# Output projection of the last 1024 rows by seven products in place of eight, behind the last attention step

## The chip, the cores and the metric

The kernel runs on one core of a Trainium2 chip (trn2). The metric is the device time of one execution in microseconds. TensorE is called PE, its weight loads PEld, VectorE DVE, ScalarE ACT, GpSimd POOL and SyncE SP. SP issues nearly all the DMAs of this kernel.

## The reference

One layer of an encoder: a norm, one input projection to queries, keys, values and a gate, a neighbourhood attention over a grid of 32 rows of 64 tokens, an output projection with a residual, and a last norm. All is float32.

```python
def rmsnorm(x, g):
    xf = x.astype(jnp.float32)
    y = xf * lax.rsqrt(jnp.mean(xf * xf, axis=-1, keepdims=True) + RMS_EPS)
    return (y * g.astype(jnp.float32)).astype(x.dtype)

# S = 2048 tokens, D = 1024, 16 heads of 64
h = rmsnorm(x, norm_0)
q, k, v, gate = jnp.split(h @ w_in_0, 4, axis=-1)
o = neighbourhood_attention(q, k, v, rpb_0)     # 8 x 16 neighbours, a bias per head and offset
x = x + (o * jax.nn.silu(gate)) @ w_out_0       # 2048 x 1024 by 1024 x 1024
out = rmsnorm(x, norm_f)
```

## The kernel before

A float32 matrix product is done in three matmuls: each operand is split into a high half h, which is the value rounded to the matmul's format (ACT copies), and a low half l = t - h (DVE subtracts), and h*h, h*l and l*h are added up in a PSUM bank. `split_to` (L433 to L439) does this.

The kernel has three parts.

1. Two stages project the input. They already multiply by seven products in place of eight: an operand is cut into four quarters, sums and differences of quarters are formed, and each of the seven products has 4 x 3 = 12 matmuls with 512 columns (`seven_products`, matmuls on L353). Several products accumulate into one bank, and DVE or ACT reads the bank out between them. POOL multiplies some results by the norm (L373).
2. The attention runs in 32 steps over (row group T, pair of heads p), `order` being T first. T is one of four groups of 512 token rows. In each step PE computes scores (s, L947), DVE adds the bias and takes the minimum of the negated score (L956), ACT takes the exponential (L961), POOL normalises (L970), PE turns the result (ph, L987), DVE and ACT copy it out (L990), PE multiplies by the values (o, L1006), and DVE multiplies by the gate (og, L1010). og is stored to a DRAM tile `ogd` and read back later with heads as rows.
3. While this chain goes on, PE is fed with other matmuls, here called fillers: `fill` (values of the second half, L846, 192 matmuls) and then `outs`, the output projection (po, L1226 to L1230). `feed(n)` takes n fillers at a time; `amount` holds how many are due in each of the steps. In the first ten steps it is 16 (with a shift between the first two), in the last 24, and in the others what the sum leaves. `feed(..., 8)` may borrow up to 4 fillers from the next step where row work was just issued (`calm`). What is left after the last step is run in a loop behind it, called the tail here.

The output projection takes 128 rows at a time (16 row tiles n) in two halves of 512 columns j: 8 k-blocks x 3 matmuls each, 48 matmuls per row tile. Around it, `load_og` reads a row tile of og, `split_og` splits it, `add_rows` adds the residual (L1108, DVE) and squares (L1111, ACT), and `finish` takes the root (L1124 DVE, L1125 and L1126 ACT), scales by root and gain (L1134, DVE) and sends the rows. The last head pair of the first two tiles of each T is not read back but split straight from og (`direct`, L1020).

Order: the program's order is written out by the code itself. `due(n)` moves a clock by matmuls, and `store(key, lag, f)` hands in work that is recorded when the clock is there. Each engine then runs its instructions in the recorded order and waits for semaphores; a DMA waits in SP's queue in the same way.

Of the kernel before, what the change touches and what calls it, by code (L numbers as in the profile page):

```python
# [23 lines left out]
NP = H // 2  # L24
# [36 lines left out]
def build(ctx, tc, x, xr, xt, wg, tab, w_out, n0, nf, out):  # L61
# [931 lines left out]
    def values(m):  # L993
# [29 lines left out]
        if p == lastp[T]:  # L1023
            store(("last", T), 2, direct)
# [60 lines left out]
    def add_rows(n, j, ps):  # L1085
        xr = RES.pop((n, j))
        state["event"] = clock[0]
        if j == 0:
            Y[n] = [], tiny.tile([128, 8], F32, name="st3")
        y, st = (raw if j else ev)([128, 512], F32, "y"), Y[n][1]  # L1090
        Y[n][0].append(y)
        if n == tiles - 1:
            cut = [slice(0, 256), slice(256, 512)] if j else [slice(0, 512)]
            for s in cut:
                nc.vector.tensor_tensor(y[:, s], ps[:, s], xr[:, s], OP.add)
            for k, s in enumerate(cut):
                to = st[:, (j if k == 0 else 5):(j if k == 0 else 5) + 1]
                nc.scalar.activation(xr[:, s], y[:, s], AF.Square, scale=0.5 ** 0.5, accum_out=to)
            if j == 0:
                nc.vector.tensor_scalar(st[:, 6:7], st[:, 0:1], 0.5 * D * EPS, None, op0=OP.add)  # L1100
            else:
                nc.vector.tensor_scalar(st[:, 7:8], st[:, 1:2], st[:, 6:7], None, op0=OP.add)
            w = (raw if j else ev)([128, 512], F32, "yw")
            nc.vector.tensor_tensor(w, y, late["nf"][j], OP.mult)
            Y[n][0][j] = w
            squared[0] += 1
            return
        nc.vector.tensor_tensor(y, ps, xr, OP.add)  # L1108

        def square():  # L1110
            nc.scalar.activation(xr, y, AF.Square, scale=0.5 ** 0.5, accum_out=st[:, j:j + 1])  # L1111
            squared[0] += 1

        store(("y", n, j), 5, square)

    def finish(n):
# [3 lines left out]
        def root():  # L1120
            if n == tiles - 1:
                nc.scalar.activation(h, st[:, 5:6], AF.Ln, bias=st[:, 7:8], scale=1.0)
            else:
                nc.vector.tensor_scalar(a, st[:, 0:1], st[:, 1:2], 0.5 * D * EPS, op0=OP.add, op1=OP.add)  # L1124
                nc.scalar.activation(h, a, AF.Ln)  # L1125
            nc.scalar.activation(r, h, AF.Exp, scale=-0.5)  # L1126

        def scale():
            if n == tiles - 1:
                nc.scalar.activation(y[0], y[0], AF.Copy, scale=r)  # L1130
                nc.vector.tensor_scalar(y[1], y[1], r, None, op0=OP.mult)
            else:
                for j in range(2):
                    nc.vector.scalar_tensor_tensor(y[j], y[j], r, late["nf"][j], op0=OP.mult, op1=OP.mult)  # L1134

        def send():
            for j in range(2):
                (nc.scalar if n == tiles - 1 and j == 0 else nc.sync).dma_start(
                    out[n * 128:n * 128 + 128, 512 * j:512 * j + 512], y[j])
# [100 lines left out]

    cycles = len(order)
# [9 lines left out]
    credit = [0.0]  # L1251
    alive = [True]

    def feed(n, calm=0):
        credit[0] += n
        while credit[0] > 0 or credit[0] > -calm_debt and clock[0] - state["event"] < calm:
# [11 lines left out]
            credit[0] -= got  # L1268
            due(got)
# [28 lines left out]
    for m in range(cycles + 1):  # L1298
# [15 lines left out]
        if m:  # L1314
            turns(m - 1)
        if m == cycles:
            all_loads()
# [13 lines left out]
    while next(outs, 0) != 0:  # L1331
        due(1)
    due(1e9)
# [31 lines left out]
```

## Time and profile before

| what | value |
|---|---|
| median of 3 runs | 1023.53 us (1023.42 to 1024.62) |
| profiled execution, its own time | 1023.25 us |
| its span, first to last instruction | 1021.4 us |
| mean granted clock of PE | 0.998 |
| PE busy | 1013.2 us, 8176 matmuls |
| DVE, ACT, POOL busy | 664.8, 474.3, 201.0 us |
| last o matmul of the attention ends | 966.06 us |
| last matmul ends | 1015.26 us |

Times are microseconds from the start of the span unless marked ns. A row of a timeline gives start, duration, engine, line, operation, output and inputs, shape and count, and in brackets the idle time before it and what ended it. Several like instructions in a row are merged to one row. A row of a group gives the count, the busy time and the mean duration in ns. A row of a stretch gives its length and each engine's busy time.

### The profile page before, as it was taken

What the parts mean: (1) busy time and instruction counts of PE and PEld (TensorE: products, weight loads), DVE (VectorE), ACT (ScalarE), POOL (GpSimd) and SP (SyncE); (2) the same over time, 40 slices, a digit from 0 to 9 for tenths busy, and PEclk for the clock granted to TensorE, in tenths of its full rate; (3) what the DMA queues carried; (4) which work ended last, traced back from release to release, by engine and by line L of the source; (5) the groups of instructions that cost most, each with busy time, mean ns of one, the idle gap of its engine ahead of it and who ended that gap; (6) DMA issues with size and microseconds to landing.
All of it is one profiled execution on the core that took longest, in us unless ns stands there. A gap on an engine that the chain in (4) does not pass through costs nothing.

```text
span 1021.4 us, 21642 instructions
## 1 busy us (share of the span) xinstructions
PE 1013.2 (99%) x8176; PEld 820.2 (80%) x8176; DVE 664.8 (65%) x1492; ACT 474.3 (46%) x1208; POOL 201.0 (20%) x341
## 2 busy tenths in 40 slices
PE   9999999999999999999999999999999999999997
PEld 7888888888888888888888877777777777877886
DVE  5385667678898795656555656667667665766543
ACT  7555323333325362332322356676666655666421
POOL 0000132232132310000000013444333332323200
PEclk9999999999999999999999999999999999999999
DMA  9633434453627244332334689899878787988442
GB/s 318 239 103 103 138 132 144 120 154 119 175 93 227 73 116 130 95 124 94 114 103 137 176 249 294 299 330 321 270 239 278 255 257 267 302 285 289 143 149 82
DMA packets 113344, 192.46 MB, mean 188 GB/s; under 512 B 10008, under 2 KB 44184, under 8 KB 113240
## 3 DMA queue, kind: packets, MB, share of 16 engines
q1 hardware_dynamic: 112808, 190.68, 58.3%
q8 instruction: 64, 1.05, 0.4%
q10 hardware_dynamic: 432, 0.40, 0.1%
q14 instruction: 40, 0.33, 0.1%
HBM read 140.71 MB, written 50.33 MB: 187 GB/s over the span
## 4 chain that ended last, share of the span: by engine, by line
PE 92%; DVE 6%; ACT 1%; issue 1%; DMA 0%; DVEq 0%; ACTq 0%
PE pp L353 42%; PE pv L477 9%; PE o L1006 8%; PE s L947 6%; PE po L1226 6%; PE po L1230 6%; PE po L1228 6%; PE ph L987 5%; PE pv L846 5%; DVE l L436 1%; DVE land L431 1%; ACT h L435 1%; DVE land L790 0%; DVE f L439 0%; DVE sixths L436 0%
## 5 line engine op out<-in xcount | busy, mean ns | idle before, releaser
L353 PE MATMUL pp<-h,f 128*128 128x512 f32 x768 | 248.5, 389 | 0.0
L970 POOL TENSOR_SCALAR x<-x,st 128x264 f32<-128x264 f32 (+1 forms) x256 | 126.3, 512 | 239.8 <-DVE st L966 237.7
L353 PEld LDWEIGHTS pp<-h,f 128*128 128x128 f32 x768 | 144.2, 188 | 29.9
L353 PE MATMUL pp<-four,f 128*128 128x512 f32 x648 | 160.8, 389 | 0.4 <-DVE u L366 0.3
L353 PE MATMUL pp<-l,f 128*128 128x512 f32 x384 | 149.4, 389 | 0.0
L353 PEld LDWEIGHTS pp<-four,f 128*128 128x128 f32 x648 | 121.4, 188 | 26.5 <-DVE u L366 1.4
L961 ACT ACTIVATE x<-x,st 128x264 f32<-128x264 f32 (+1 forms) x256 | 124.4, 487 | 21.1 <-DVE st L956 21.1
L373 POOL TENSOR_TENSOR tmp<-tmp,rb 128x512 f32<-128x512 f32 x36 | 59.2, 1647 | 268.3 <-DVE tmp L371 224.9
L990 DVE COPY pta<-ph 120x512 f32<-120x512 f32 (+5 forms) x96 | 56.0, 638 | 71.5 <-PE ph L987 71.4
L1226 PE MATMUL po<-woh,gh 128*128 128x512 f32 x240 | 94.8, 395 | 0.0
L1230 PE MATMUL po<-wol,gh 128*128 128x512 f32 x240 | 94.4, 394 | 0.0
L1228 PE MATMUL po<-woh,gl 128*128 128x512 f32 x240 | 94.0, 392 | 0.0
L956 DVE CUSTOM_DVE_ANT_0 x<-s,em 128x264 f32<-128x264 f32 (+1 forms) x256 | 90.7, 408 | 2.1 <-PE s L947 1.8
L1006 PEld LDWEIGHTS o<-pta,vt 120*64 120x64 f32 (+2 forms) x1024 | 68.5, 137 | 19.9 <-DVE st L956 12.3
L353 PEld LDWEIGHTS pp<-l,f 128*128 128x128 f32 x384 | 72.1, 188 | 15.0
L1006 PE MATMUL o<-pta,vt 120*64 120x192 f32 (+5 forms) x1024 | 83.4, 316 | 0.0
L990 ACT ACTIVATE pta<-ph 120x512 f32<-120x512 f32 (+5 forms) x96 | 48.0, 558 | 75.2 <-PE ph L987 75.2
L436 DVE TENSOR_TENSOR f<-raw,f 128x512 fp32r<-128x512 f32 x80 | 55.1, 690 | 28.3 <-ACT f L435 28.3
L361 ACT ACTIVATE p<-pp 128x512 f32<-128x512 f32 x24 | 14.3, 597 | 122.6 <-PE pp L353 122.6
L435 ACT ACTIVATE f<-raw 128x512 fp32r<-128x512 f32 x80 | 49.3, 626 | 32.9 <-PE pp L353 12.5
L947 PE MATMUL s<-kt,qt 64*32 64x264 f32 (+1 forms) x2048 | 64.2, 374 | 0.0
L477 PE MATMUL pv<-wh,h 128*128 128x512 f32 x192 | 63.9, 393 | 0.0
(155 smaller groups left out, 1600.6 us busy)
## 6 DMA issues: line engine op xcount, KB each, us to landing
raw<-in_wg_dram SPq DMA_DIRECT2D x124, 256.0 KB, 4.3
em<-in_tab_dram SPq DMA_DIRECT2D x16, 912.0 KB, 7.6
em<-in_tab_dram SPq DMA_DIRECT2D x16, 528.0 KB, 7.2
vd<-v SPq DMA_DIRECT2D x32, 256.0 KB, 2.6
sgd<-sg SPq DMA_DIRECT2D x32, 256.0 KB, 3.2
qt<-qd SPq DMA_DIRECT2D x32, 256.0 KB, 5.4
sgt<-sgd SPq DMA_DIRECT2D x32, 256.0 KB, 7.7
ogd<-og SPq DMA_DIRECT2D x32, 256.0 KB, 2.6
```

The costliest lines, as they stand in the source:

```text
L353: nc.tensor.matmul(B[n, P], t[:, int(m == 2), c], x[k][int(m == 1)], start=P in (1, 6, 5) and k == 0 and m == 0, stop=k == 3 and m == 2, s ...
L436: nc.vector.tensor_tensor(l, t, h.bitcast(F32), OP.subtract)
L477: nc.tensor.matmul(ps[t], a[:, o], b, start=k == 0 and m == 0, stop=k == NK - 1 and m == 2)
L947: nc.tensor.matmul(pst[s][h * 32:h * 32 + 32], qt[e, q:q + 32], keys.rearrange("p r (s c) -> p s r c", c=8), start=True, stop=True)
L956: nc.vector.tensor_tensor_reduce(X[i, C][s], ps, em, -1.0, 1e38, OP.add, OP.min, st[:, o:o + 1])
L961: nc.scalar.activation(X[i, C][s], X[i, C][s], AF.Exp, bias=st[:, o:o + 1], scale=-1.0, accum_out=st[:, 4 + o:5 + o])
L970: nc.gpsimd.tensor_scalar(X[i, C][s], X[i, C][s], st[:, o:o + 1], 1.0, op0=OP.mult, op1=OP.mult)
L990: (nc.vector.tensor_copy if h else lambda o, i_: nc.scalar.activation(o, i_, AF.Copy))(to[:k, :, 2 - j, h, c], at[h][:k, :, c])
L1006: nc.tensor.matmul(o[s * 64:s * 64 + 64, g0 * 64:g1 * 64 + 64].rearrange("d (g q) -> d g q", q=64), vt[:k, strip, s * 64:s * 64 + 64], t[: ...
L1226: nc.tensor.matmul(p, gh, woh[q, j], start=(i == 0), stop=False)
L1228: nc.tensor.matmul(p, gl, woh[q, j], start=False, stop=False)
L1230: nc.tensor.matmul(p, gh, wol[q, j], start=False, stop=(i == NK - 1))
```

## The change

The rows of the last two groups T (1024 rows) are taken out of the row tiles (`tiles` goes from 16 to 8). They are projected in a new tail by seven products: n is one of four blocks of 256 rows, A11 to A22 are quarters of the block's activations (128 rows by 512 heads-columns), B11 to B22 quarters of the weight for one k-block. S1 to S4 are sums of A quarters (on POOL), T1 to T4 sums of B quarters (on POOL or DVE, from raw weights that are loaded again), and each sum is split in high and low half. A product P has 12 matmuls; products 1 and 2 share a bank, 6, 7 and 4 share one, 5 and 3 share one. Each bank is read out between them (`evac_o`): by ACT for P = 1, by DVE otherwise, and POOL adds a partial sum to the residual rows. `amount` gives fewer fillers to each step from the eleventh to the thirty-first. `direct` is no longer used: all 8 head pairs are read back. The weights' first sums are loaded and formed in the last four steps (`before_end`, `after_turns`).

```diff
-        if p == lastp[T]:
+        if False:
             store(("last", T), 2, direct)
-    tiles = S // 128
+    tiles = S // 256
-        return NK - 1 if i < 2 else NK
+        return NK
...
+    order_t = [(0, 1), (1, 1), (0, 2), (1, 2), (2, 1),
+               (0, 6), (2, 2), (0, 7), (0, 5), (0, 4), (0, 3),
+               (1, 6), (3, 1), (1, 7), (1, 5), (1, 4), (1, 3),
+               (2, 6), (3, 2), (2, 7), (2, 5), (2, 4), (3, 6), (2, 3),
+               (3, 7), (3, 5), (3, 4), (3, 3)]
...
+    def sum_w(k, f, e):
+        b = RW[k]
+        to, x_, y_, o = {"T3": ("B22", "B22", "B12", OP.subtract), "T1": ("B12", "B12", "B11", OP.subtract),
+                         "T2": ("B11", "B11", "B22", OP.add), "T4": ("B21", "B21", "B11", OP.subtract)}[f]
+        e.tensor_tensor(b[to], b[x_], b[y_], o)
...
+    def sum_a(n, f):
+        a, b, o = {"S1": ("A21", "A22", OP.add), "S2": ("S1", "A11", OP.subtract),
+                   "S3": ("A11", "A21", OP.subtract), "S4": ("A12", "S2", OP.subtract)}[f]
+        A[n, f] = get2() if f in ("S1", "S2") else A[n, {"S3": "A21", "S4": "A12"}[f]]
+        nc.gpsimd.tensor_tensor(A[n, f], A[n, a], A[n, b], o)
+
+    def form_a(n, P):
+        F[n, P] = t = freer.pop(0) if freer else wp([128, 2, 512], F32R, "f")
+        split_to(t[:, 0], t[:, 1], A[n, uses[P][0]], None)
+
+    def product_o(n, P):
+        if P in (1, 6, 5):
+            B[n, P] = bank(512, "pt")
+            for Q in {1: (2,), 6: (7, 4), 5: (3,)}[P]:
+                B[n, Q] = B[n, P]
+        t = F.pop((n, P))
+        for k in range(4):
+            c = slice(k * 128, k * 128 + 128)
+            for m in range(3):
+                nc.tensor.matmul(B[n, P], t[:, int(m == 2), c], WO[uses[P][1], k][int(m == 1)],
+                                 start=P in (1, 6, 5) and k == 0 and m == 0, stop=k == 3 and m == 2,
+                                 skip_group_check=True)
+                due(1)
+        freer.append(t)
...
+    def evac_o(n, P):
+        p = B[n, P]
+        if P == 1:
+            U[n, 1] = get2()
+            nc.scalar.activation(U[n, 1], p, AF.Copy)
+        elif P == 2:
+            nc.vector.tensor_tensor(R[n, 0, 0], p, R[n, 0, 0], OP.add)
+            nc.gpsimd.tensor_tensor(R[n, 1, 0], R[n, 1, 0], U[n, 1], OP.add)
+            square_o(n, 0, 0)
...
+        elif P == 6:
+            U[n, 2] = get2()
+            nc.vector.tensor_tensor(U[n, 2], p, U[n, 1], OP.add)
+            nc.gpsimd.tensor_tensor(R[n, 0, 1], R[n, 0, 1], U[n, 2], OP.add)
+        elif P == 7:
+            U[n, 3] = U[n, 2]
+            nc.vector.tensor_tensor(U[n, 3], p, U[n, 1], OP.add)
+            nc.gpsimd.tensor_tensor(R[n, 1, 1], R[n, 1, 1], U[n, 3], OP.add)
+            free2.append(U[n, 1])
+        elif P == 5:
+            nc.vector.tensor_tensor(R[n, 1, 1], p, R[n, 1, 1], OP.add)
+            square_o(n, 1, 1)
+            free2.append(U[n, 3])
...
+    def after_turns():
+        ts = [xp([128, 512], F32, "raww") for _ in range(8)]
+        load_raw_w(1, ts[:4])
+        load_raw_w(2, ts[4:])
+
+    def tail():
...
+        for n in range(4):
...
+            at(at_[6] - 60, sum_a, n, "S1")
+            at(at_[6] - 52, sum_a, n, "S2")
+            at(max(at_[6] - 44, at_[2] - 20), sum_a, n, "S4")
+            at(at_[6] - 30, sum_a, n, "S3")
+            for P in range(1, 8):
+                at(max(at_[P] - 23, 1), form_and_free, n, P)
...
+        while next(outs, 0) != 0:
+            due(1)
+        for n, P in order_t:
+            product_o(n, P)
+            evac_o(n, P)
+        due(1e9)
-    amount += [(192 + 546 - sum(amount) - first - end_of_it) / (cycles - 10)] * (cycles - 10) + [end_of_it]
+    amount += [(192 + 384 - 33 - sum(amount) - first - end_of_it) / (cycles - 10)] * (cycles - 10) + [end_of_it]
```

More of the change, by code (lines that the diff above doesn't have):

```diff
@@ L1091, in add_rows @@
         Y[n][0].append(y)
[L1092 to L1107, printed above, removed]
         nc.vector.tensor_tensor(y, ps, xr, OP.add)
@@ L1251, in build @@
     credit = [0.0]
+    fed = [0]
     alive = [True]
@@ L1330, in build @@
     store(("roots",), 8, run_roots)
-    while next(outs, 0) != 0:
-        due(1)
-    due(1e9)
+    tail()
 def kernel(**inputs):
```

166 lines of the change are left out of this document (153 added, 13 removed).

## The prediction

> **What bounds the kernel now.** I read the page's busy shares first, then stretches of the span, then single steps in order of time.
>
> ```profile
> PE 1013.2 (99%) x8176; PEld 820.2 (80%) x8176; DVE 664.8 (65%) x1492; ACT 474.3 (46%) x1208; POOL 201.0 (20%) x341
> PE 92%; DVE 6%; ACT 1%; issue 1%; DMA 0%; DVEq 0%; ACTq 0%
> ```
>
> PE is busy for 99% of the span and holds 92% of the chain that ended last. A matmul taken off PE is worth its full time, as long as the others keep up.
>
> The stretches below have PE, PEld, DVE, ACT and POOL busy time, then the granted clock, the DMA share and GB/s.
>
> ```profile
> 640.00:700.00 60.00, 59.64 (x965) 46.68 (x964) 40.82 (x145) 42.73 (x135) 25.72 (x58) 1.00 0.95 322
> 720.00:850.00 130.00, 130.00 (x1855) 101.99 (x1852) 87.42 (x285) 80.05 (x259) 44.26 (x89) 1.00 0.80 261
> 954.80:966.00 11.20, 11.20 (x111) 8.93 (x111) 3.31 (x6) 2.92 (x9) 2.82 (x7) 1.00 0.54 177
> 966.00:1015.30 49.30, 49.26 (x218) 40.46 (x216) 20.32 (x36) 12.82 (x37) 0.00 (x0) 1.00 0.36 118
> 1015.30:1021.40 6.10, 0.00 (x0) 0.00 (x0) 2.06 (x5) 2.12 (x7) 0.00 (x0) 0.68 0.22 86
> ```
>
> The attention steps (720 to 850) leave PE no idle time. From 966 the tail runs 216 filler matmuls (two records of the o product share the count): 49.2/216 = 0.228 us each. That start-to-start time is the price of a matmul; the mean of one, 389 ns, overlaps the next. The tail has DVE at 41% and POOL at nothing. After the last matmul 6.1 us of norm and output remain.
>
> **What the change removes.** The last 1024 rows cost 8 tiles x 48 = 384 matmuls; seven products cost 4 x 7 x 12 = 336. Saved: 48 x 0.228 = **10.9 us**. That is all PE can give. The order has 735 fillers inside the attention before and 540 now; behind it 216 before and 363 now. So the steps lose 195 x 0.228 = 44.4 us and the tail gains 147 x 0.228 = 33.5. What matters is whether the shorter steps and the denser tail keep PE fed.
>
> **The shorter steps.** One step, PE and POOL in order of time:
>
> ```profile
> 823.83 2.61 PE L1006 MATMUL o<-pta,vt 120*64 120x128 f32 x32
> 832.03 1.62 PE L987 MATMUL ph<-ident,x 64*120 64x64 f32 x48
> 825.69 3.79 POOL L970 TENSOR_SCALAR x<-x,st 128x264 f32<-128x264 f32 x8 [7.94 <-DVE st L966]
> 781.23 2.67 POOL L970 TENSOR_SCALAR x<-x,st 128x264 f32<-128x264 f32 x4 [0.79 <-DVE st L1124]
> 784.92 1.62 PE L987 MATMUL ph<-ident,x 64*120 64x64 f32 x48
> ```
>
> Between o (ends 826.44) and the turns at 832.03 stand 24 fillers. POOL's normalising ends at 829.48, so 2.55 us is spare. The new order puts 11 to 19 fillers there (15 on average) in the 22 steps before the last. Nine fewer take 2.05 us: 0.5 spare. In the five steps with 11 to 13, up to thirteen fewer take 3.0: PE waits about 0.3 on average. In a step disturbed by row work (the last two rows) POOL ends at 783.90, and 1.0 us is spare; nine fewer would leave PE waiting 1.0. Five short steps at 0.3 give 1.5; the row work thins with the fillers, and four steps hold 18 or 19 to cover it, so I add half a microsecond for what is left uncovered: **+2 us**. Lower end 0.5: the steps at 640 to 700 held 13 to 20 fillers and lost 0.36. Upper end 5: one disturbed step per row tile in these steps, seven at 0.7.
>
> **The tail: a port that POOL and DVE cannot use at once.** Before, POOL's queue ends with the last normalising:
>
> ```order
> L970 TENSOR_SCALAR x0_5119<-x0_5119,st_11209 128x3x88
> L970 TENSOR_SCALAR x1_5121<-x1_5121,st_11209 128x3x88
> L970 TENSOR_SCALAR x0_5171<-x0_5171,st_11238 128x3x64
> L970 TENSOR_SCALAR x1_5172<-x1_5172,st_11238 128x3x64
> L970 TENSOR_SCALAR x0_5182<-x0_5182,st_11238 128x3x64
> L970 TENSOR_SCALAR x1_5183<-x1_5183,st_11238 128x3x64
> L1360 UNCONDITIONAL_BRANCH
> ```
>
> Now 33 additions follow; these are the first (raww: raw weights, og2 and og4: quarters of the activations, t2: scratch and residual):
>
> ```order
> L970 TENSOR_SCALAR x1_5183<-x1_5183,st_10940 128x3x64
> L1246 TENSOR_TENSOR raww_11079<-raww_11079,raww_11077 128x512
> L1246 TENSOR_TENSOR raww_11077<-raww_11077,raww_11076 128x512
> L1246 TENSOR_TENSOR raww_11076<-raww_11076,raww_11079 128x512
> L1278 TENSOR_TENSOR t2_11198<-og2_10885,og2_10886 128x512
> L1278 TENSOR_TENSOR raww_10331<-t2_11198,og4_10889 128x512
> L1278 TENSOR_TENSOR og4_10889<-og4_10889,raww_10331 128x512
> L1278 TENSOR_TENSOR og2_10885<-og4_10889,og2_10885 128x512
> L1352 TENSOR_TENSOR t2_11153<-t2_11153,raww_10331 128x512
> L1246 TENSOR_TENSOR raww_11078<-raww_11078,raww_11076 128x512
> ```
>
> All moved from nowhere else: new work, on two SBUF operands each. The trace shows such additions beside DVE work at one place (DVE first, then POOL):
>
> ```profile
> 348.46 1.67 DVE L790 TENSOR_TENSOR land<-land,spot 128x512 f32<-128x512 f32 x1
> 350.16 1.67 DVE L791 TENSOR_TENSOR spot<-spot,land 128x512 f32<-128x512 f32 x1
> 351.75 1.78 DVE L789 TENSOR_TENSOR land<-land 128x512 f32<-128x512 f32 x1
> 355.26 0.69 DVE L791 TENSOR_TENSOR spot<-spot,land 128x512 f32<-128x512 f32 x1
> 355.87 0.68 DVE L789 TENSOR_TENSOR land<-land 128x512 f32<-128x512 f32 x1
> 359.51 4.08 DVE L436 TENSOR_TENSOR sixths<-land,sixths 128x512 fp32r<-128x512 f32 x3
> 349.66 1.62 POOL L790 TENSOR_TENSOR land<-land 128x512 f32<-128x512 f32 x1
> 351.36 1.62 POOL L791 TENSOR_TENSOR land<-land 128x512 f32<-128x512 f32 x1
> 352.94 1.74 POOL L797 TENSOR_TENSOR land<-land,spot 128x512 f32<-128x512 f32 x1
> 267.98 0.68 DVE L371 TENSOR_TENSOR tmp<-pp,u 128x512 f32<-128x512 f32 x1
> 267.60 3.31 POOL L373 TENSOR_TENSOR tmp<-tmp,rb 128x512 f32<-128x512 f32 x2 [3.52 <-DVE tmp L371]
> ```
>
> Alone, DVE starts such a row every 0.61 us (355.26 to 355.87). Beside POOL it starts one every 1.70 (348.46 to 350.16): the row waits until POOL's ends (351.28), then runs. Each POOL addition so costs DVE 1.1 us where DVE's next row has both inputs in SBUF, as splits, weight sums and scalings have. A row whose first input is PSUM escapes: L371 at 267.98 (pp is a bank) took its usual 0.68 in the midst of POOL's addition from 267.60.
>
> DVE's queue up to the product that comes eighth, (0,7), before (the end of the tail) and now (L436: low half of a split; wol, four, sixths: weights; f: activations; pt: banks):
>
> ```order
> L1108 TENSOR_TENSOR y_11525<-po_11495,xr_11422 128x512
> L1077 TENSOR_TENSOR gl_11534<-ograw_11453,gh_11533 128x512 x2
> L1124 TENSOR_SCALAR st3_11492<-st3_11492 128x1
> L1134 SCALAR_TENSOR_TENSOR y_11493<-y_11493,st3_11492,acc0_165 128x512
> L1134 SCALAR_TENSOR_TENSOR y_11525<-y_11525,st3_11492,acc1_166 128x512
> L1108 TENSOR_TENSOR y_11569<-po_11527,xr_11465 128x512
> ```
>
> ```order
> L1351 TENSOR_TENSOR t2_11188<-pt_11230,t2_11188 128x512
> L436 TENSOR_TENSOR f_11133<-t4_11166,f_11133 128x512
> L436 TENSOR_TENSOR wol_7304<-t2_11157,woh_7303 128x512
> L1246 TENSOR_TENSOR raww_11074<-raww_11074,raww_11072 128x512
> L436 TENSOR_TENSOR four_11116<-raww_11074,four_11116 128x512
> L436 TENSOR_TENSOR f_11172<-og2_10885,f_11172 128x512
> L436 TENSOR_TENSOR four_11120<-raww_11078,four_11120 128x512
> L436 TENSOR_TENSOR sixths_11121<-t2_11158,sixths_11121 128x512
> L1360 TENSOR_TENSOR raww_11072<-pt_11338,raww_10331 128x512
> ```
>
> Before, seven such rows come per 48 matmuls, 10.9 us; now 42 stand within 25. The last row reads the bank (pt_11338) that (0,7) adds to, so (0,7) cannot start before it.
>
> PE without waits reaches (0,7) after 27 fillers and seven products, 111 x 0.228 = 25.3 us behind the last o. DVE has the og product (0.7) and then 42 rows to that evacuation: 24 splits and 7 sums at 0.61 = 18.9; 5 PSUM reads at 0.61 = 3.0; 4 scalings at 0.75 = 3.0 and two small ones 0.3.
>
> ```profile
> L1134 DVE SCALAR_TENSOR_TENSOR y<-y,st,acc 128x512 f32<-128x512 f32 x10 | 7.1, 749 | 2.5 <-ACT st L1126 2.5
> L1108 DVE TENSOR_TENSOR y<-po,xr 128x512 f32<-128x512 f32 x8 | 5.5, 690 | 19.7 <-PE po L1230 19.7
> L1111 ACT ACTIVATE xr<-y 128x512 f32<-128x512 f32 x8 | 5.0, 630 | 25.2 <-DVE y L1108 25.2
> L1111 ACT ACTIVATION_READ_ACCUMULATOR xr<-y 128x1 f32 x8 | 1.5, 187 | 0.0
> L1126 ACT ACTIVATE st<-st 128x1 f32<-128x1 f32 x6 | 1.2, 203 | 0.2
> ```
>
> Together 25.9: DVE alone would be 0.6 late. Eleven POOL additions stand ahead of that point: 11 x 1.1 = 12.1 more, 9.1 if the five PSUM reads hide under them. So (0,7) is 0.6 (nothing collides) to 12.7 late. DVE has no idle time there to give, and the rows are those of 348 to 363, so I take a value near the upper end: **+10 us**.
>
> From there to the end PE needs 252 matmuls, 57.4 us. DVE has 63 rows: 20 splits, a multiplication and 20 evacuations at 0.61 = 25.0, 14 scalings 10.5, 8 small ones 1.2, 36.7; POOL's other 22 additions 24.2: 60.9 if all collide, 48.7 if every evacuation hides one. So it nearly fits; waits in a fixed order (a scaling waits for ACT's root with the next split behind it) add some: **+2.5**, ends 0 and 6.
>
> The end: the other row group's add, square, root and scaling now fall inside the last product: 0.69 + 0.63 + 0.19 + 0.2 + 0.41 + 1.55 = 3.7 against 12 x 0.228 = 2.7, and the last evacuation stands behind them on DVE: **+1**, ends 0 and 1.5.
>
> SP's loads of four raw weight blocks and of a stored quarter go out in the steps before, under DMA at 0.54 (954.80); POOL's four early sums fall in its idle 7.9 us between two steps' normalising. Both cost nothing; uncovered, a load is part of the stalls above.
>
> **Sum**: -10.9 + 2 + 10 + 2.5 + 1 = +4.6. The profiled execution took 1023.25 (span 1021.4), so 1027.9; the median is 0.3 higher: **1028.2 us**, its own range 1024.5 to 1034.
>
> **Rivals.** (1) The port costs little: POOL's sums fall where DVE reads PSUM or waits for PE, and the tail follows PE. Then -10.9 + 2 + 2 (for 0.6 to 4 late) + 0 + 0.5 = -6.4, **1017**. For it: stage one ran 36 such additions without PE idling. Against: DVE had room there, here it has none until (0,7). Deciding point: whether (0,7) starts within 4 us of its place. (2) The steps become bound by the chain scores, exp, normalising, turns; DMA rises too (0.95 at 640 to 700). With half a microsecond lost in each of 22 steps, 11 in place of 2: **1037**; if the tail also goes well, 1026. (3) PE's clock: in the last 6.1 us without matmuls the clock averages 0.68, so it falls soon after idling starts. If stalls of over 3 us in the tail bring it down,
>
> ```profile
> 1.19 3.59 PE L114 MATMUL zp<-z 128*128 128x512 bf16 x8 [1.19 <-DVE z L111]
> ```
>
> matmuls go at about 0.43 us (3.59 for 8, as at the start), a product takes 5.2 in place of 2.7. Two products that DVE does not hide: +5, **1033**.
>
> The rule for it is in the Trainium skill, "TensorE: Matmul & The Clock Gate", Part 1: an idle window of about 3.4 us halves the clock, a busy one restores it. By it one long stall in the tail would cost at most about 1.7 us, an estimate from that page.
>
> (4) The saving isn't there: no, the order counts 48 matmuls fewer.
>
> **Chances.** Forecast 0.52, (1) 0.30, (2) 0.09, (3) 0.09. A measurement here tells 0.2%, 2 us, from none. Faster: nearly all of (1) and a corner of the forecast, 0.31. Same: the forecast's low edge and mixtures, 0.09. Slower: 0.60. The range 1015.5 to 1035 takes in (1), the forecast and (3), and leaves out the tails of (1) and (2).
>
> **What will show it.** Right: no PE idle ahead of the attention; some tenths of PE idle in steps with 11 fillers; in the tail DVE rows of 1.7 us beside POOL additions, and PE idle some 10 us before (0,7). Wrong: DVE at 0.61 per row there with POOL busy; (0,7) on time; or PE idle mainly in the steps.

## The result and the profile after

The changed kernel takes **1061.0 us** (1059.1 to 1062.4, four runs) beside 1023.5 for the kernel before: ratio 1.0363, interval 1.0345 to 1.0381. Slower was forecast, but by 4.7 us and not by 37.5, and 1061 lies far outside the range. The profiled execution took 1062.38, its span 1060.6, which is 39.2 more than before.

Two rows of the page of the changed kernel, the busy times and the chain of work that ended last:

```profile
PE 1019.7 (96%) x8128; PEld 818.4 (77%) x8128; DVE 705.5 (67%) x1531; ACT 490.2 (46%) x1236; POOL 261.3 (25%) x378
PE 76%; DVE 9%; issue 4%; POOL 4%; ACT 4%; DMA 3%; SPq 1%; POOLq 0%; ACTq 0%; DVEq 0%
```

The 48 matmuls are gone (8128 for 8176), yet PE's busy time has grown, and the chain that ended last now runs through PE for 76% of the span in place of 92%. Stretches of the changed kernel, with the columns that the prediction explains:

```profile
687.80:707.00 19.20, 14.07 (x165) 9.88 (x166) 6.89 (x25) 8.63 (x28) 4.94 (x13) 0.82 0.72 240
720.00:850.00 130.00, 128.32 (x2068) 98.39 (x2067) 92.77 (x319) 87.50 (x285) 55.41 (x106) 1.00 0.89 286
936.90:966.00 29.10, 20.36 (x79) 15.77 (x80) 25.17 (x27) 8.43 (x20) 16.31 (x10) 0.88 0.55 205
966.00:1000.00 34.00, 27.96 (x106) 21.45 (x104) 21.22 (x31) 14.41 (x32) 13.02 (x9) 0.90 0.30 101
1000.00:1052.20 52.20, 46.24 (x180) 36.65 (x180) 30.92 (x49) 16.95 (x45) 21.97 (x14) 0.90 0.28 91
1052.20:1060.60 8.40, 0.01 (x1) 0.00 (x0) 2.97 (x7) 2.13 (x7) 0.00 (x0) 0.77 0.33 125
```

One attention step (687.8 to 707) loses 5.1 us of PE's time at a clock of 0.82. The other steps lose little each. The tail (from 936.9, where the last o ends) is where most goes: DVE is busy for 25.2 of its first 29.1 us while PE works for 20.4, and the granted clock is 0.88 to 0.90. The end is 8.4 long; it was 6.1. What PE waited for in the tail (microseconds in all, times, longest):

```profile
PE pt L1293 <- ACT raww L1349: 7.5, 1, 7.5
PE pt L1293 <- DVE raww L1360: 3.9, 1, 3.9
PE pt L1293 <- DVE t L1360: 2.8, 2, 2.1
PE pt L1293 <- ACT t L1349: 2.7, 1, 2.7
PE pt L1293 <- ACT f L435: 2.6, 1, 2.6
PE pt L1293 <- DVE f L436: 1.2, 1, 1.2
```

L1349 is ACT's read-out of a bank behind a product 1, L1360 DVE's behind a product 6. Up to product (0,7) the forecast named DVE alone; behind it, it named scalings that wait for ACT's root.

Where the 39.2 us are, from the trace: -10.9 for the matmuls; 8.4 in the one step; some 7 in other steps; 20.4 in the tail up to (0,7), which starts 45.7 behind the last o and not 25.3; 12.2 from there to the last matmul (69.6 us for 252 matmuls that need 57.3); 2.2 at the end. The experiments say what each of these is.

### The profile page after: what moved, and what is told of

Same layout as the page of the kernel before. It is cut to its first block, busy times and chain, and to the rows that moved or that the text cites. A ratio compares the mean times of both kernels' runs of the same rounds, so it can differ in the third digit from the quotient of the medians.

```text
span 1060.6 us, 21744 instructions
## 1 busy us (share of the span) xinstructions
PE 1019.7 (96%) x8128; PEld 818.4 (77%) x8128; DVE 705.5 (67%) x1531; ACT 490.2 (46%) x1236; POOL 261.3 (25%) x378
## 3 DMA queue, kind: packets, MB, share of 16 engines
q1 hardware_dynamic: 115688, 195.40, 57.4%
## 4 chain that ended last, share of the span: by engine, by line
PE 76%; DVE 9%; issue 4%; POOL 4%; ACT 4%; DMA 3%; SPq 1%; POOLq 0%; ACTq 0%; DVEq 0%
PE pp L353 40%; PE pv L477 8%; PE o L1006 6%; PE s L947 6%; PE ph L987 4%; PE pv L846 4%; PE po L1204 2%; PE po L1202 2%; PE po L1206 2%; POOL x L970 2%; ACT x L961 1%; DVE f L436 1%; DMA ogd<-og 1%; DVE l L436 1%; POOL raww L1278 1%
## 5 line engine op out<-in xcount | busy, mean ns | idle before, releaser
L970 POOL TENSOR_SCALAR x<-x,st 128x264 f32<-128x264 f32 (+1 forms) x256 | 130.3, 528 | 201.2 <-DVE st L966 200.3
L990 ACT ACTIVATE pta<-ph 120x512 f32<-120x512 f32 (+5 forms) x96 | 47.7, 558 | 57.4 <-PE ph L987 57.4
L947 PE MATMUL s<-kt,qt 64*32 64x264 f32 (+1 forms) x2048 | 67.3, 382 | 5.1 <-ACT pta L990 5.1
L371 DVE TENSOR_TENSOR tmp<-pp,u 128x512 f32<-128x512 f32 x48 | 33.1, 690 | 47.3 <-PE pp L353 42.7
L477 PE MATMUL pv<-wl,h 128*128 128x512 f32 x192 | 63.3, 389 | 0.0
L477 PE MATMUL pv<-wh,l 128*128 128x512 f32 x192 | 63.2, 389 | 0.0
```

The source lines that it names most:

```text
L477: nc.tensor.matmul(ps[t], a[:, o], b, start=k == 0 and m == 0, stop=k == NK - 1 and m == 2)
L947: nc.tensor.matmul(pst[s][h * 32:h * 32 + 32], qt[e, q:q + 32], keys.rearrange("p r (s c) -> p s r c", c=8), start=True, stop=True)
L970: nc.gpsimd.tensor_scalar(X[i, C][s], X[i, C][s], st[:, o:o + 1], 1.0, op0=OP.mult, op1=OP.mult)
L990: (nc.vector.tensor_copy if h else lambda o, i_: nc.scalar.activation(o, i_, AF.Copy))(to[:k, :, 2 - j, h, c], at[h][:k, :, c])
```

## The experiments

Times are medians; "+" is the difference from the kernel before, measured along with each group of runs: 1023.5 us for e1 to e8 and 1024.4 to 1024.9 for the others. e2, e4, e5 and e13 leave out most columns of POOL's sums, e6 the weight sums, and in e9, e11 and e15 some sums are of other numbers; the other runs compute everything.

| run | us | beside before | ratio, interval |
|---|---|---|---|
| the change | 1061.0 | +37.5 | 1.0363, 1.0345 to 1.0381 |
| e1 first row tile | 1053.1 | +29.6 | 1.0290, 1.0260 to 1.0320 |
| e2 POOL narrow | 1048.7 | +25.2 | 1.0247, 1.0217 to 1.0277 |
| e3 sums on DVE | 1054.9 | +31.4 | 1.0308, 1.0278 to 1.0338 |
| e4 e1 and e2 | 1041.0 | +17.5 | 1.0172, 1.0140 to 1.0204 |
| e5 e4 kept warm | 1038.8 | +15.4 | 1.0149, 1.0119 to 1.0178 |
| e6 e4, no weight sums | 1029.0 | +5.6 | 1.0050, 1.0030 to 1.0069 |
| e7 short steps alone | 1030.5 | +7.1 | 1.0068, 1.0045 to 1.0090 |
| e8 last group only | 1026.3 | +2.9 | 1.0030, 1.0018 to 1.0043 |
| e9 e8 reordered | 1020.2 | -4.2 | 0.9956, 0.9944 to 0.9969 |
| e10 e1, squares late | 1040.8 | +16.4 | 1.0165, 1.0149 to 1.0180 |
| e11 e9 again | 1019.4 | -5.3 | 0.9952, 0.9940 to 0.9965 |
| e12 e10, read-outs first | 1039.7 | +15.1 | 1.0150, 1.0137 to 1.0164 |
| e13 e12, POOL narrow | 1029.0 | +4.4 | 1.0051, 1.0036 to 1.0067 |
| e14 e9 with S4 early | 1019.8 | -5.1 | 0.9955, 0.9943 to 0.9968 |
| e15 e12, no raw loads | 1034.5 | +9.6 | 1.0095, 1.0081 to 1.0109 |
| e16 e12, all on DVE | 1036.6 | +11.7 | 1.0111, 1.0095 to 1.0126 |

### e1: the first row tile

Rows of the changed kernel about the lost step, of SP's queue (first two), ACT and PE:

```profile
688.53 0.53 SPq L1013 DMA_DIRECT2D ogd<-og  x1
692.34 0.32 SPq L1063 DMA_DIRECT2D ograw<-ogd  x1
698.18 1.15 ACT L1076 ACTIVATE gh<-ograw 128x512 fp32r<-128x512 f32 x2 [9.07 <-DMA ograw<-ogd]
699.76 3.86 PE L947 MATMUL s<-kt,qt 64*32 64x264 f32 x62 [5.13 <-ACT pta L990]
```

With `direct` gone, the first row tile needs all eight head pairs from DRAM. The last is stored at 688.53 and the load is issued at 692.34, and ACT's split of that tile stands in its queue ahead of the copies of the turns (pta). ACT waits 9.07 us, and PE behind it.

```diff
-        if False:
+        if p == lastp[T] and T == 0:
             store(("last", T), 2, direct)
...
-        return NK
+        return NK - 1 if T == 0 and i < 2 else NK
```

> Undoes one part of the change: the first two row tiles again read back 7 head pairs and split the eighth straight from og (direct, for T = 0 alone). Theory F (the first row tile now waits for the last head pair's way through DRAM, and ACT's queue waits with it): the 8 us of PE idle near 690 to 702 go, 1061 becomes 1052 to 1054. Rival (that stall is a start-up accident of the T change, and the missing time shows up in the next steps): less than 3 us gained.

Measured: 1053.1, 8 us less. The step's loss is the missing `direct`, an edit that stands in the diff of the change and that the prediction did not price.

### e2, e3, e4: the port

In the changed kernel's tail, DVE (first three) and POOL:

```profile
942.39 3.49 DVE L1111 SCALAR_TENSOR_TENSOR y<-y,st,acc 128x512 f32<-128x512 f32 x2
945.80 1.76 DVE L436 TENSOR_TENSOR f<-og,f 128x512 fp32r<-128x512 f32 x1
947.49 4.20 DVE L1246 TENSOR_TENSOR raww<-raww 128x512 f32<-128x512 f32 x3
941.80 5.22 POOL L1246 TENSOR_TENSOR raww<-raww 128x512 f32<-128x512 f32 x3 [13.35 <-DMA raww<-in_w_out_dram]
946.98 1.73 POOL L1278 TENSOR_TENSOR t<-og,og 128x512 f32<-128x512 f32 x1
```

Two scalings take 3.49 beside POOL (the prediction's rows give 0.75 each without it) and a split 1.76 in place of 0.68, as forecast. Three runs put a price on it; e2 narrows POOL's additions to 8 of 512 columns (S1 and S2 are set to zero first), e3 gives them to DVE whole, e4 is e1 and e2 together.

```diff
+        w = slice(0, 8) if e is nc.gpsimd and ended[0] else slice(0, 512)
-        e.tensor_tensor(b[to], b[x_], b[y_], o)
+        e.tensor_tensor(b[to][:, w], b[x_][:, w], b[y_][:, w], o)
...
-            nc.gpsimd.tensor_tensor(R[n, 0, 1], R[n, 0, 1], U[n, 2], OP.add)
+            nc.gpsimd.tensor_tensor(R[n, 0, 1][:, :8], R[n, 0, 1][:, :8], U[n, 2][:, :8], OP.add)
```

```diff
-        nc.gpsimd.tensor_tensor(A[n, f], A[n, a], A[n, b], o)
+        nc.vector.tensor_tensor(A[n, f], A[n, a], A[n, b], o)
```

> The 33 POOL additions of the tail work on 8 of 512 columns (the sums' other columns are left out, S1 and S2 are set to zero first), so the order and every wait stay, only POOL's time goes. Theory L (the port that POOL and DVE share makes the tail late): the tail loses 33 us to waits now, and 25 of them go: about 1036. Rival Q (DVE and ACT have too many rows in a fixed order and wait for each other, POOL or no POOL): 10 us or less go, 1051 or more.

> All 33 additions of the tail run on DVE in place of POOL, whole. Theory L: DVE has 33 rows x 0.61 = 20 us more, but none waits 1.1 us for the port (33 x 1.1 = 36): some 8 to 15 us faster than the change, about 1050. Rival Q (DVE's row count decides): 10 us or more slower, 1070.

> The two edits of the first and second run together (8 columns of each POOL addition in the tail; the rest of the sums left out). If the two losses are separate and L holds, 1061 - 8 - 25 = 1028; by Q, 1043 or more. What is then still above 1023.5 - 10.9 = 1012.6 belongs to the shorter steps (some 6 us) and to the queues' order.

Measured: e2 12.3 us less than the change, between the two theories; e3 6.1 less, where 8 to 15 were expected; e4 20 less, the sum of e1 and e2. So narrowing the additions takes away about a third of the loss, and with it and the first row tile away the kernel was still 17.5 over before.

### e5: the clock

Five products in the changed kernel's tail come behind a wait of PE and run in part at the halved clock; they take 4.61, 4.86, 4.58, 5.46 and 4.18 us where the others take 2.88: 9.3 us in all. e5 is e4 with useless matmuls for PE where two such waits are.

```diff
+            if (n, P) in ((0, 2), (2, 2)):
+                q = bank(512, "warm")
+                for _ in range(14):
+                    nc.tensor.matmul(q, woh[0, 0][:, :128], woh[0, 0], start=True, stop=True)
```

> The fourth run's kernel (first row tiles as before, POOL's tail additions on 8 columns, the rest of the sums left out) with 14 matmuls of no use put ahead of products (0,2) and (2,2), where PE idled 3.4 us each and then ran a product at half clock (5.5 us in place of 2.9). Theory C (the clock that falls in a wait costs time of its own): the products run at full clock, 2 x 2.6 = 5 us are gained, 1041 becomes 1036. Rival (a product at half clock is hidden, the next wait is as much shorter): 1041, within 2.

Measured: 2.1 us less than e4, with intervals of 3 us to either side of each: between the two, and not clear of noise. In the trace the two products are 4.9 us shorter (5.49 us each in e4) and (0,7) starts only 1.6 earlier, so a slow product seems mostly to take time that PE would else have waited.

### e6: the weights

```diff
-        for t, f, *a in ((1, split3, 0, "T2"), (5, split3, 0, "T3"), ... (100, done_w, 3)):
-            at(t, f, *a)
+        for k in range(4):
+            for f, (q, c) in (("T2", (k, 0)), ("T3", (k, 1)), ("T1", (4 + k, 0)), ("T4", (4 + k, 1))):
+                WO[f, k] = woh[q, c], wol[q, c]
```

> The fourth run's kernel without loading, summing and splitting the raw weights for T1 to T4 (their places hold the plain weights' halves instead, so the products are others). Theory Q1 (the weights' 25 rows in the first third of the tail make it late): (0,7) starts 25 to 27 us behind the last o in place of 37.4, 1041 becomes 1029. Rival Q2 (the lateness comes from the order of evacuations, squares and roots in DVE's and ACT's queues): less than 4 us gained; the 2.2 us waits before (1,7) and (2,7) belong to Q2 and should stay in either case.

Measured: 1029.0, another 12 us. (0,7) starts 25.2 behind the last o, in its place, and the waits of 2.1 us before (1,7) and (2,7) stay. The preparation of the weight sums holds up the tail's start; this run does not tell whether by their loads, their number or their place in the queues. e10 to e16 do.

### e7: the short steps alone

The kernel before, with the change's number of fillers in each step and the rest behind the last step as plain row tiles (all 8176 matmuls).

```diff
-        if p == lastp[T]:
+        if p == lastp[T] and T == 0:
...
-    amount += [(192 + 546 - sum(amount) - first - end_of_it) ...
+    amount += [(192 + 351 - sum(amount) - first - end_of_it) ...
```

> The kernel before, with the change's number of fillers in each step (11 to 19 in place of 24) and the rest, 411 plain matmuls, in the tail; every row by eight products (only the first group's eighth head pair is split straight from og). Theory S (the step's own chain from scores to turns is longer than its fillers): it loses what the change lost there, 5 to 6 us: 1029. Forecast of the prediction: 2 us. Rival (the loss in the steps comes from the new loads and sums in them): 1023 to 1025.

Measured: +7.1. In e7 (PE's waits on POOL in the whole run, then one step, PE and POOL):

```profile
PE ph L987 <- POOL x L970: 2.4, 4, 0.9
771.71 1.67 PE L987 MATMUL ph<-ident,x 64*120 64x64 f32 x42 [0.54 <-POOL x L970]
767.37 4.74 POOL L970 TENSOR_SCALAR x<-x,st 128x264 f32<-128x264 f32 x8 [6.80 <-DVE st L966]
```

The mechanism is the one forecast: the turns wait for POOL's normalising, which takes 4.74 here beside row work on DVE and 3.79 in the step of before. A step takes about 6.2 us besides its fillers at 0.2275 each; six steps, with 11 to 15 fillers and row work, take 0.6 to 2.1 more, 6.6 in all. PE's plain waits show only part of it, the matmuls around them come further apart too.

### e8: seven products for the last group only

To see whether the steps' and the tail's losses go together, e8 takes only the last 512 rows by seven products (24 matmuls saved, 5.5 us), keeps 140 plain fillers in the tail as cover for the weights, and does weight and residual sums on DVE.

```diff
-    tiles = S // 256
+    tiles = 3 * S // 512
...
-        for n in range(4):
+        for n in (2, 3):
...
-    amount += [(192 + 384 - 33 - sum(amount) ...
+    amount += [(192 + 576 - 147 - sum(amount) ...
```

> Seven products for the last group alone (512 rows, 168 matmuls in place of 192), 21 fillers more per three steps than the change, 140 plain matmuls and then the products in the tail, so that the weights are prepared behind plain matmuls; weights' and residual sums on DVE; the two blocks' products interleaved. It saves 24 x 0.228 = 5.5 us. If weights, chain and queues are what cost the change its time, at most 3 us go back: 1018 to 1021, faster than before. If the port alone decides, POOL's 8 sums cost little here too, the same. If products cannot be fed at all at this rate: 1026 or more.

Measured: 1026.3, above the 1018 to 1021 expected, and the number given for products that cannot be fed at this rate; e9 shows that they can. The steps hold some 19 fillers and lose nothing (the last o ends at 939.84, 0.2 late). The tail loses 4.8 and the end 4.1. Two rows of e8, DVE and PE:

```profile
1003.22 0.69 DVE L436 TENSOR_TENSOR f<-t,f 128x512 fp32r<-128x512 f32 x1 [1.37 <-ACT f L435]
986.08 1.92 PE L1298 MATMUL pt<-four,f 128*128 128x512 f32 x4 [1.79 <-DVE f L436]
```

DVE idles 1.3 to 1.4 us before each of the last four splits (ACT's rounding of the same operand comes just ahead of it). This led to the theory of the next runs.

### e9, e10: the order of ACT's queue

The same place in the changed kernel, between products (3,1) and (1,7): DVE (three rows), ACT (three) and PE:

```profile
997.59 0.68 DVE L1378 TENSOR_TENSOR raww<-pt,raww 128x512 f32<-128x512 f32 x1
999.58 0.69 DVE L436 TENSOR_TENSOR f<-raww,f 128x512 fp32r<-128x512 f32 x1 [1.31 <-ACT f L435]
1002.24 0.68 DVE L1360 TENSOR_TENSOR raww<-pt,raww 128x512 f32<-128x512 f32 x1
998.31 0.63 ACT L1304 ACTIVATE t<-raww 128x512 f32<-128x512 f32 x1 [2.08 <-DVE raww L1378]
998.84 0.19 ACT L1304 ACTIVATION_READ_ACCUMULATOR t<-raww 128x1 f32 x1
998.94 0.61 ACT L435 ACTIVATE f<-raww 128x512 fp32r<-128x512 f32 x1
1003.07 4.18 PE L1293 MATMUL pt<-four,f 128*128 128x512 f32 x9 [3.87 <-DVE raww L1360]
```

DVE reads a bank out (997.59). ACT, idle for 2.08, squares that row (998.31), and only then rounds the operand of a later product (998.94), which it could have done long before. DVE's low half waits for that (1.31 idle), and behind it stands DVE's next read-out, L1360, for which PE waits 3.87. It is a ring through three engines that the code writes out by calling `square_o` inside `evac_o`, before the next split is due. e10 is e1 with the square put off by two matmuls and the root behind it by one; e9 is e8 with it, the sums S on DVE, T1's splits later and block 2 finished first.

```diff
-        nc.scalar.activation(junk[0], R[n, a, c], AF.Square, scale=0.5 ** 0.5, accum_out=STF[n, a][:, c:c + 1])
+        y, st = R[n, a, c], STF[n, a]
+        store(("q",), 2, lambda: nc.scalar.activation(junk[0], y, AF.Square, scale=0.5 ** 0.5, accum_out=st[:, c:c + 1]))
...
-        store(("y", n, a), 6, root)
+        store(("y", n, a), 7, root)
```

> The kernel of the run before this one in the table (seven products for the last 512 rows only, 24 matmuls saved, 5.5 us) with its queues reordered and nothing left out: each square is recorded two matmuls later, so that ACT's next split stands ahead of it; the sums S go from POOL to DVE, so that POOL has no row in the tail; the splits of T1 come later; product (3,2) stays next to last and the products of block 2 are finished first. There the tail lost 4.8 us and the end 4.1. Theory Q2 (these losses come from the fixed order of the queues and from POOL's port, and not from the amount of work): the waits of 1.3 us of DVE for ACT's splits go, no stall of PE over 1 us is left, the end is within 1.5 us of before: 1019 to 1021.5, faster than the kernel before by 2 to 4.5 us. Rival (the tail of seven products is bound by the amount of DVE's and ACT's work, in whatever order): 1024 to 1027, no better than the run it comes from.

> The change with the first row tile kept direct, as in the first experiment (1053.1), and each square of the tail recorded two matmuls later, the root one later: nothing else, the same work on every engine, nothing left out. Theory Q2: behind product (0,7) what makes PE wait is a ring in the fixed order: DVE reads a bank out, ACT squares it, ACT's next high half stands behind the square, DVE's low half behind that (1.31 to 1.38 us of idle DVE each time), and DVE's next read-out behind that; with the squares behind the splits these waits go, the gaps ahead of (1,7) and (2,7) (3.9 and 2.1 us, and the half clock behind them, about 1.7 each) go or shrink to under 1: 1045 to 1049. Rival (the port, or the amount of work, delays these read-outs): within 1.5 us of 1053.

Measured: e10 1040.8, 13 us nearer to before than e1, more than expected; e9 1020.2, as expected. In e10, DVE, then ACT, and the stretch from (0,7) to the last matmul:

```profile
984.60 0.68 DVE L1379 TENSOR_TENSOR raww<-pt,raww 128x512 f32<-128x512 f32 x1
985.20 0.68 DVE L436 TENSOR_TENSOR f<-raww,f 128x512 fp32r<-128x512 f32 x1
983.14 0.62 ACT L435 ACTIVATE f<-raww 128x512 fp32r<-128x512 f32 x1
971.60:1030.30 58.70, 58.07 (x252) 46.95 (x252) 42.85 (x62) 23.42 (x59) 32.78 (x21) 1.00 0.29 99
```

The rounding now comes ahead, DVE's split follows its read-out at once, and the 252 matmuls take 58.6 us, 1.3 over their 57.3, where e1 lost 11.2. The additions on POOL are all still there (32.78 busy), so the port alone did not hold this part up. The port made the ring dearer: with the squares early and POOL narrow (e4) the same 252 matmuls lose 7.3 us, against 11.2 in e1. (0,7) starts 42.9 behind the last o in place of e1's 45.6.

### e12 to e16: what made (0,7) late

In the changed kernel ACT, and PE behind it, ahead of product (0,2):

```profile
951.72 0.63 ACT L435 ACTIVATE four<-raww 128x512 fp32r<-128x512 f32 x1 [8.11 <-DVE raww L1246]
957.04 0.58 ACT L1349 ACTIVATE raww<-pt 128x512 f32<-128x512 f32 x1
957.67 0.79 PE L1293 MATMUL pt<-woh,f 128*128 128x512 f32 x1 [7.46 <-ACT raww L1349]
```

ACT stands 8.11 us at the split of a weight sum, and its read-out of (0,1), for which PE waits 7.46, is queued behind it. e12 is e10 with those splits behind the read-outs; e13 is e12 with e2's narrow additions; e15 is e12 without the loads of the raw weights of two blocks; e16 is e12 with e3's edit.

```diff
-  (26, split3, 1, "T2"), (30, split3, 1, "T3"), ... (40, split3, 2, "T2"), (44, split3, 2, "T3")
+  (46, split3, 1, "T2"), (47, split3, 1, "T3"), ... (58, split3, 2, "T2"), (59, split3, 2, "T3")
```

```diff
-        e.tensor_tensor(b[to], b[x_], b[y_], o)
+        x_, y_ = (RW[0]["B22"], RW[0]["B12"]) if k in (1, 2) else (b[x_], b[y_])
+        e.tensor_tensor(b[to], x_, y_, o)
...
-        load_raw_w(1, ts[:4])
-        load_raw_w(2, ts[4:])
```

> e10 (1040.8) with the splits of the weight sums of blocks 1 to 3 (T2 and T3) recorded 3 to 20 matmuls later, behind ACT's read-out of products (0,1) and (1,1); same work, nothing left out. In e10 PE still waited 7.4 us ahead of (0,2) and 3.0 ahead of (2,2) for ACT's read-out of a bank, with ACT standing at the split of a weight sum that was not formed yet, for 7.6 us. Theory Q2 (order): the 7.4 shrinks to 2 or less, (0,7) starts at 36 to 38 behind the last o in place of 42.9, and the time is 1034 to 1037. Rival P (the raw weights land late, POOL waited 13.9 us for them, and the port; the splits are late wherever they stand, and PE now waits for the weights ahead of (0,6)): (0,7) at 41 or later, 1039 to 1042.

> e12 with the 33 additions on POOL in the tail done on 8 of their 512 columns, so that they hold the port hardly at all (what they leave out is not computed). In e2 this was worth 12.4 us with the squares ahead of the splits. Theory L (each POOL addition costs DVE 1.1 us and DVE has none to spare until (0,7), as the prediction had it): 8 to 12 us below e12, (0,7) within 4 us of its place at 25.3. Theory Q2 (the port only hurt because a row that is late holds up others in the fixed order): 3 to 6 us below e12.

> e12 (1039.7) without the eight loads of the raw weights of blocks 1 and 2: their sums read two tiles of block 0 instead (so these sums are of other numbers), the same sums and splits on the same engines. In e12 POOL stood 14.4 us until these loads landed, and (0,7) was 16.4 us late, of which e13 gave 10.5 to the port. Theory W (the other 6 are the late landing of the raw weights, which the prediction took as free): 4 to 7 us below e12, 1033 to 1036. Rival (it is the number of sums and splits, not when they can start): within 1.5 us of e12.

> e12 with the 33 additions of the tail on DVE in place of POOL, whole, nothing left out. The port is then free, and DVE has 33 rows of 0.61 more. Theory L (each POOL addition costs DVE 1.1 us up to (0,7)): 11 x (1.1 - 0.61) = 5.4 less there, about nothing behind it: 1033 to 1036. Rival (POOL's additions hide under DVE's reads of banks and its waits, and DVE is full): 1038 or more.

Measured. **e12**: 1.3 us nearer to before than e10, which is not clear of noise: the rival. PE's wait ahead of (0,2) falls from 7.4 to 5.4, and 1.8 of it comes back inside (2,1) and (0,6); (0,7) starts at 41.7. What ACT waited for is late wherever its wait stands. In e12, SP, POOL and DVE:

```profile
924.45 4.22 SPq L1240 DMA_DIRECT2D raww<-in_w_out_dram  x8
934.82 4.84 POOL L1246 TENSOR_TENSOR raww<-raww 128x512 f32<-128x512 f32 x3 [14.38 <-DMA raww<-in_w_out_dram]
938.44 5.13 DVE L1246 TENSOR_TENSOR raww<-raww 128x512 f32<-128x512 f32 x3
```

**e13**: 10.7 us less than e12, as the port's theory said, and (0,7) 10.5 earlier. At 31.3 it is still 6.0 late, where that theory allowed 4. The same three sums on DVE in e13, and the stretch from the last o to (0,7) in e12 and in e13:

```profile
936.74 2.17 DVE L1247 TENSOR_TENSOR raww<-raww 128x512 f32<-128x512 f32 x3
928.86:970.59 41.73, 30.15 (x112) 22.51 (x112) 37.32 (x44) 17.45 (x38) 19.30 (x13) 0.88 0.57 201
928.62:959.88 31.26, 26.33 (x112) 20.48 (x112) 26.25 (x44) 17.10 (x38) 6.58 (x16) 1.00 0.75 267
```

5.13 to 2.17: 1.0 us a row, as forecast (1.1). The same 44 rows of DVE are busy for 11.1 us less, and DVE idles no less than before (4.4 us, then 5.0). So the 10.5 is time that DVE's rows lost beside POOL, and not that POOL's results came sooner; and e13's other theory (the port hurts only through the order) falls for this part. In e2, with the squares still early, the same edit made (0,7) 9.0 earlier and the rest of the tail 5.1 shorter.

**e15**: 5.5 us nearer to before than e12, inside the 4 to 7 expected, and (0,7) 5.4 earlier. The eight loads can't be issued before the last turns free their tiles (924.45), and land so late that POOL's first sum starts at 934.82; without them it starts at 923.55, eleven us earlier:

```profile
923.55 3.77 POOL L1247 TENSOR_TENSOR raww<-raww 128x512 f32<-128x512 f32 x3 [4.12 <-PE ph L987]
```

**e16**: 3.4 us nearer than e12, between the theories: (0,7) comes 2.1 earlier, where 11 rows at 1.1 less 0.61 would give 5.4. PE still waits 4.6 and 4.3 us ahead of (0,2) and (2,2) for ACT's read-outs; why not more is gained is not shown.

### e11, e14: a version that is faster than both

By an oversight e11 ran e9's kernel once more, unchanged; its text speaks of e14's. In e9 the last S4 reads a tile that by then holds another value; e14 forms it while its source is still there.

```diff
-            at(max(at_[6] - 42, at_[2] - 20), sum_a, n, "S4")
+            at(at_[6] - 42 if n == 3 else at_[2] - 20, sum_a, n, "S4")
```

> The kernel of e9 with one difference: the sum S4 of block 3 is formed some 75 matmuls earlier, while the tile of S2 that it reads still holds S2 (in e9 that tile had been given to another value by then, so that S4 there was a sum of other numbers, at the same work). Theory Q2 (losses of a seven-product tail come from the fixed order of the queues, and are gone here): as e9, 1019 to 1021.5, faster than before by 2 to 4.5 us. Rival (the earlier row displaces DVE's splits and the gain is lost): 1023 or more.

> What e11 was to be (by an oversight e11 ran e9's kernel once more, unchanged): e9 with the sum S4 of block 3 formed some 75 matmuls earlier, while the tile that it reads still holds S2; everything that the reference asks for is computed. Theory Q2 (the losses of a seven-product tail came from the fixed order of the queues and from POOL's port, and are gone here): as e9, 1019 to 1021.5, faster than before by 2 to 4.5 us. Rival (the earlier row displaces DVE's splits): 1023 or more.

Measured: e14 1019.8 us, ratio 0.9955 (0.9943 to 0.9968), with all of the output. Of e14 the busy times, PE's longest wait in the tail, the tail and the end:

```profile
PE 1008.0 (99%) x8152; PEld 814.9 (80%) x8152; DVE 697.4 (69%) x1541; ACT 486.9 (48%) x1229; POOL 214.9 (21%) x345
PE pt L1298 <- DVE raww L1366: 0.6, 1, 0.6
941.20:1011.20 70.00, 69.42 (x306) 56.84 (x304) 57.34 (x96) 29.59 (x72) 0.00 (x0) 1.00 0.48 168
1011.20:1018.00 6.80, 0.21 (x1) 0.00 (x0) 2.71 (x7) 2.13 (x7) 0.00 (x0) 0.89 0.23 88
```

PE is back at 99%, POOL has no row in the tail, the clock is 1.00 and the end 6.5. The 24 matmuls are worth 5.5 us, and 3.4 of the span's 1021.4 are gained.

## Why the prediction failed

The direction was right, the sum was not. Three terms were too small (the steps, the tail up to (0,7), the rest of the tail), the first row tile had none, and within the tail the loads were put at nothing. What the prediction had right, the matmuls (-10.9) and the port (+10.5), about cancel; the 37.5 come from losses that it had too small or not at all, so that the sign came out right is partly luck. Term by term, in us of the span:

| term | forecast | measured | shown by |
|---|---|---|---|
| 48 matmuls at 0.228 | -10.9 | -10.9 | matmul count |
| first row tile without `direct` | no price | +8 | e1 |
| shorter steps | +2 | +7 | e7 |
| tail up to (0,7) | +10 | +20.4 | port 10.5 (e13), raw loads 5.4 (e15), squares 2.7 (e10), read-outs 1.1 (e12) |
| rest of the tail | +2.5 | +12.2 | squares 9.9 (e10, in part together with the port) |
| the end | +1 | +2.2 | trace |

The parts of a row come from runs in turn, each taken against the one it is built on; that they add up elsewhere was seen once (e4). The 1.1 of e12 is not clear of noise.

**The first row tile** is the plainest miss. The prediction gave the `direct` edit no price; `parts(n)` changed for the first group too, where the first row tile is needed a few us after its last head pair is stored. The diff and the order of ACT's queue held what was needed to see it: a load behind that store, and the split of the loaded tile ahead of the turns.

**The steps**: the mechanism (POOL's normalising ends after the turns could start) and the places (11 fillers, row work) were as forecast, the size was not. The prediction took 0.3 us for a short step from an average of spare times, and half a microsecond for row work, since that thins with the fillers. Where a short step and row work still meet, POOL's normalising itself gets longer (4.74 for 3.79), and the step loses up to 2.1. Rival (2), with 11 in place of 2, was as near as the forecast in size, but it spread the loss over 22 steps, and six had it.

**The port** was priced right: 10 forecast, 10.5 by e13. But the 10 stood for the whole lateness of (0,7), which was 20.4. Rival (1) is out. The Trainium skill says in "SBUF — State Buffer", section "SBUF: two separate sides", that POOL and a DVE row with two SBUF inputs take the shared pair as an exclusive lock; the three sums above, 5.13 beside POOL and 2.17 without, agree.

**The loads**: that the loads of the raw weights cost nothing was wrong by 5.4. Of the four blocks only the first is loaded steps ahead; two are issued behind the last turns (`after_turns`). The prediction looked at how busy the DMA was (0.54) and not at when the tiles become free: a load into a tile that the last step still uses can't be issued before that step's turns, and the tail begins 4 us later.

**The order of the queues** cost 2.7 + 1.1 + 9.9, and it is the largest step of the prediction that failed. For the rest of the tail the prediction summed DVE's rows (60.9) against PE's time (57.4) and took them to nearly fit. e10 leaves every row, POOL's additions too, and shows that they do fit (1.3 lost); what doesn't is the ring read-out, square, rounding, low half, next read-out. The prediction named a wait of that kind (a scaling for ACT's root) and gave it 2.5. It added up no rows of ACT, which is busy for 46% of the span, and did not ask what stands ahead of what in its queue; the order of ACT's rows had to be read there as DVE's was.

**The clock** (rival 3) did fall, at five products, by 9.3 us of PE's time, and as far as e5 shows little of it is time of the kernel. It follows the waits.

**The end**: right in kind. The last read-out starts 0.9 behind the last matmul, since the other row group's root and scalings stand ahead of it. e14, with the squares behind the splits and product (3,2) ahead of the last, ends in 6.5.

## What to carry to other kernels

Where engines run fixed queues, sum up no engine's rows before you have followed one round of the dependency through every queue that it passes: one kind of row, written two matmuls too early on an engine that is half idle, cost 13 us here. A load is priced by when its target becomes free, not by the bandwidth left. And when a change removes a special case, price it at each place where the case applied, not only at the one that the change is about.

## What the runs showed of the hardware

The clock doesn't follow the length of a wait alone. Of the changed kernel (a PE row, the 3.41 us up to where the clock falls, and the next 3.41), then of e10 (the same three):

```profile
1024.48 2.90 PE L1293 MATMUL pt<-four,f 128*128 128x512 f32 x9 [2.08 <-DVE t L1360]
1022.57:1025.98 3.41, 1.50 (x7) 1.27 (x8) 2.96 (x5) 0.65 (x2) 1.57 (x1) 1.00 0.62 189
1025.98:1029.39 3.41, 3.41 (x10) 2.63 (x9) 2.70 (x3) 1.46 (x4) 3.41 (x4) 0.50 0.13 41
```

```profile
967.40 0.50 PE L1293 MATMUL pt<-woh,f 128*128 128x512 f32 x1 [3.01 <-ACT t L1350]
962.85:966.27 3.42, 1.54 (x7) 0.94 (x5) 3.35 (x6) 1.94 (x6) 0.00 (x0) 1.00 0.85 275
966.27:969.68 3.41, 2.28 (x10) 1.89 (x11) 2.48 (x4) 3.16 (x6) 1.01 (x1) 1.00 0.89 318
```

A wait of 2.08 us was followed by a clock of 0.50, 1.5 us after the next matmuls had begun; one of 3.01 left it at 1.00. In every trace of this case the granted clock changes only on a grid of 3.41 us. Every stretch of that grid at full clock in which PE idled for more than 57% was followed by the half clock, none with less than 47% was, and between the two both happened (51 of 5332 stretches were so followed). The wait of 2.08 fell almost whole into one stretch (56% idle); the wait of 3.01 was parted by the grid (55% and 33%). The Trainium skill's rule in "TensorE: Matmul & The Clock Gate", Part 1, that the activity is judged in windows of about 3.4 us that run freely, fits both; that a whole idle window is needed does not fit the first. The five slow products took 1.3 to 2.6 us longer, beside the 1.7 that the prediction had worked out from that page as the most; around the slowest, (1,7), the clock was at half for two stretches in a row (1002.08 to 1008.91).

The port slows POOL too: three sums take 3.77 us in e15, where DVE has no row with two SBUF inputs just then (it ends its copies out of PSUM at 924.6 and is idle to 927.9), and 5.22 in the changed kernel, 0.5 more a row.
